# Leading products of a two-layer encoder kernel on x without token factors, splits in landing order, norms written tile by tile

## The chip, the cores and the metric

The kernel runs on one core of a Trainium2 chip. The metric is the device time of one execution in microseconds (us), the median of several. The core has five engines, each with a queue of its own: TensorE (PE; weight loads are shown apart as PEld), VectorE (DVE), ScalarE (ACT), GpSimd (POOL) and SyncE (SP, which here only issues DMAs). SBUF is the on-chip memory, PSUM the accumulators that TensorE writes.

## The reference

Two encoder layers on x, 512 tokens of 1024 channels, in float32. What matters here is the start of each layer:

```
mem_n = rms_norm(mem, mem_norm_g)                      # 256 memory tokens
for l in range(2):
    h = rms_norm(x, g_pre_mix[l])                      # x * rsqrt(mean(x*x) + eps) * g
    proj = h @ w_in[l]                                 # 1024 x 5632
    q_a, k_a, v_a, q_b, k_b, v_b, q_m, gate_pre = split(proj)
    o_a = neighborhood_attention(q_a, k_a, v_a, rpb[l])      # 6 heads
    o_b = dilated_attention(q_b, k_b, v_b)                   # 6 heads
    o_m = memory_attention(q_m, mem_n, w_mem_kv[l])          # 4 heads; kv = mem_n @ w_mem_kv
    merged = sum of three gated branch projections
    x = x + rms_norm(merged @ w_out[l], g_post_mix[l])
    h = rms_norm(x, g_pre_ffn[l])
    u = depthwise_conv(h @ w_up[l]); a, b = split(u)
    x = x + rms_norm((gelu(a) * b) @ w_down[l], g_post_ffn[l])
```

rms_norm is a product of one factor per token (the reciprocal root, "token factor" below), one per channel (g) and x. The token factor can be applied before a product or to its result, since a product with weights mixes channels and not tokens.

## The kernel before, in words

**Layout.** x lies in SBUF transposed, as eight tiles of 128 channels x 512 tokens (`x[k]`), and is worked on in two halves of 256 tokens (`HALVES`). Every product is three matmuls: each operand is split into a high part (fp32r, a ScalarE cast) and the remainder, the low part (a subtraction), and hi·hi, lo·hi and hi·lo are summed in PSUM (`mm3`, all products at L242). In the trace a weight is `wraw` (as loaded, three buffers), `whi` and `wlo` (two buffers each) or, for the leading products, tiles `m`. All operations of ScalarE and VectorE go through one helper and so carry line L114; they are told apart by the names of their tiles. GpSimd's own subtractions are L220, the weight DMAs L225.

**Order of the work.** TensorE's order is fixed by hand: the class `Woven` (L46) chains each matmul behind the one before. Pieces of the kernel are generators ("jobs"), spawned with a delay on a modelled TensorE clock; between products `tick` runs the jobs that are due, `give` and `need` set and await flags, so a job's matmuls fall between the products of the main line. The other engines work off their queues in the order that a scheduler derives; an operation that waits holds up all behind it on its engine.

**The start of layer 0** (L834 to L870). `load_x` (L190) brings half 0 of x in four DMAs, then two weights, then half 1. `first_squares` (L825) has ScalarE square the tiles and VectorE add them; `rstd_job` (L321) turns the sums into token factors: matmuls with `mean` (128x1, into `pt`), a root on ScalarE, a reciprocal on VectorE, and matmuls with `ident` that spread the factors over 128 partitions of a PSUM bank. `pre_norm_job` (L359) then makes eight normed tiles of a half (`normed`, L340: x · g · factor, then the split into `h`) and gives one flag for all eight. `run_group` (L466) multiplies with the six leading weights `FIRST = (0, 3, 6, 1, 4, 7)`, two by two, half 0 and then half 1, into six PSUM banks: mm, mm, s, s, o, pt (288 matmuls of 256 columns).

**Behind it.** `mem_kv` (L444) multiplies the normed memory tokens (`mem_norm_job`, L416, which also needs `mean`, a root and a spread) by four weights, 96 matmuls, with two copies of the results each. Then the loop over `pr`: for pr 0 and 1 the six results of the group are evacuated by `a_q`, `a_k`, `a_v` (L528 to L549: scale and split into `m`, into the padded key tiles `ka`, and into the value tile `sq`), for pr = 2 three more projections (`proj`, L480) are made. `attention_job` (L731) weaves the heads in between. PSUM has three mm banks, two s, two pt and one o.

**The boundary between the layers.** `end_job` (L373) finishes layer 0 half by half: residual adds and square sums per tile, then, after a pause of 9.0, `pre_norm_job` of layer 1. `run_group` of layer 1 waits for the flag of the whole half.

Of the kernel before, what the change touches and what calls it, by code (L numbers as in the profile page):

```python
# [7 lines left out]
F32 = mybir.dt.float32  # L8
# [111 lines left out]
def tile_hybrid_encoder(ctx, tc, xT, memT, memg, vecs, rpb, w_in, w_kv, w_bra, w_brb, w_brm,  # L120
# [18 lines left out]
    def nm(s):  # L139
        uid[0] += 1  # L140
        return f"{s}_{uid[0]}"
# [48 lines left out]
    def load_x(half):  # L190
        for k in range(0, KD, 2):
            nc.sync.dma_start(out=xs[k // 4][:, k % 4:k % 4 + 2, half], in_=xT[:, k:k + 2, half])

    load_x(HALVES[0])
    eps = const.tile([128, 1], F32, name="eps")
    nc.gpsimd.memset(eps, RMS_EPS)
    ACT.activation(smalls(1), eps, AF.Sqrt)
# [21 lines left out]
        last_copy[0] = ACT.copy(hi, src).ins  # L219
        last_lo[eng or V] = (eng or V).tensor_sub(lo, src, f32(hi)).ins  # L220

    def weights(src, K, C, slot=None, eng=None, after=None):

        raw = wp.tile([128, K, C], F32, tag="wraw", name=nm("wraw"))
        nc.sync.dma_start(out=raw, in_=src)  # L225
        if slot is None:
            hi = wp.tile([128, K, C], F32R, tag="whi", name=nm("whi"), bufs=2)
            lo = wp.tile([128, K, C], F32R, tag="wlo", name=nm("wlo"), bufs=2)
            split(raw, hi, lo, eng)
            behind(last_copy[0], after)  # L230
            return [(hi[:, k, :], lo[:, k, :]) for k in range(K)]
        n = 512 // C
        w = []
        for k in range(0, K, n):
            c = min(n, K - k)
            hi, lo = slot(F32R, (128, c, C)), slot(F32R, (128, c, C))
            split(raw[:, k:k + c, :], hi, lo, eng)
            w += [(hi[:, i, :], lo[:, i, :]) for i in range(c)]
        return w
# [105 lines left out]
    def raw_split(l, goff, k, src, hi, lo):  # L345

        g = vec[:, l, goff + k:goff + k + 1]
# [25 lines left out]
    def end_job(l, goff, og, acc, acc2, i, then, lat, more=()):  # L373
        half, box = HALVES[i], []
        yield lat
        yield from rstd_job([acc[:, half]] + list(more), 256, box)
        for k in range(KD):
            V.tensor_mul(og[k][:, half], og[k][:, half], box[0])
            (G if then is None and i and k in TAILG else V).tensor_add(x[k][:, half], x[k][:, half], og[k][:, half])
            if acc2 is not None:  # L380
                sumsq_add(acc2[:, half], x[k][:, half], k == 0, None, G if k in SQG[goff == V_POSTF] else V)
            else:
                nc.sync.dma_start(out=out[:, k, half], in_=x[k][:, half])
        if then is not None:
            yield 9.0
            yield from then(i)

    def factor_end_job(l, goff, og, acc, acc2, i, nxt):

        half, box = HALVES[i], []  # L390
        gnext, h, R = nxt
        yield ready(1.4)
        yield from rstd_job([acc[:, half]], 256, box)
        for k in range(KD):
            V.tensor_mul(og[k][:, half], og[k][:, half], box[0])
            V.tensor_add(x[k][:, half], x[k][:, half], og[k][:, half])
            raw_split(l, gnext, k, x[k][:, half], h[k][0][:, half], h[k][1][:, half])
# [62 lines left out]
    def group_weights(srcs, engs):  # L460
        return [weights(s, KD, 128, big, e) for s, e in zip(srcs, engs)]

    def group_banks():
        return [mmbank(), mmbank(), sbank(), sbank(), obank(128), tbank()]

    def run_group(grp, hs, half, flag, cols=None, side=2):  # L466
        if flag and side == 2:
            wv.need(flag)
        n = len(hs)
        ws, pss = grp  # L470
        for i in range(0, len(ws), side):
            for k in range(n):
                if flag and side > 2:
                    wv.need(f"{flag}.{k}")
                rhs = [t[:, half] for t in hs[k]]
# [356 lines left out]
                V.tensor_add(sqs[k], sqs[k], sqs[k - 2])  # L832
        return sqs[5::2]

    hs = h_tiles()
    wv.spawn(pre_norm_job(0, V_PRE, first_squares(HALVES[0]), hs, 0))
    gw = group_weights([w_in[0, m] for m in FIRST[:2]], (V, G))
    load_x(HALVES[1])
    wv.need(f"h0.{V_PRE}.0")
    with tc.issue_after(last_copy[0]):  # L840
        sqs = first_squares(HALVES[1])
    wv.spawn(pre_norm_job(0, V_PRE, sqs, hs, 1), SD1)
    gw += group_weights([w_in[0, m] for m in FIRST[2:]], (V, G, V, G))
    for t, c in ((mask, c_mask), (tab0, c_tab0), (tab1, c_tab1)):
        nc.sync.dma_start(out=t, in_=c)
    hm = []
    wv.spawn(mem_norm_job(0, hm, big), 6.0)
    km, vm = [], []

    for l in range(depth):  # L850
        pss = group_banks()
        for i in range(2):
            run_group((gw, pss), hs, HALVES[i], f"h{l}.{V_PRE}.{i}")
# [85 lines left out]
        if l == depth - 1:  # L939
            sublayer_end(l, V_POSTF, w_of, fs, 2, None)  # L940
            while wv.jobs:
                wv._step()
        else:
            hm, km, vm = [], [], []
            wv.spawn(mem_norm_job(l + 1, hm, htile))
            box, pre = [], []

            def then(a, i, l=l, box=box):
                if i == 0:
                    box.extend(h_tiles())  # L950
                return pre_norm_job(l + 1, V_PRE, a, box, i)

            gw = []

            def kv_ahead(l=l, pre=pre, gw=gw):
                pre.append(weights(w_kv[l + 1, 0], KD, 128, htile))
                yield KVD
                for i in (1, 2, 3):
                    yield 0.9
                    pre.append(weights(w_kv[l + 1, i], KD, 128, big, G if KVE[i] == 'G' else V))  # L960
                wv.give(f"kv{l + 1}")
                for m in range(NG):
# [9 lines left out]
            wv.need(f"h{l + 1}.{V_PRE}.0")  # L972
            hs = box


# [91 lines left out]
```

## Time and profile before

| | |
|---|---|
| runs | 1562.01, 1562.01 and 1564.1 us, median 1562.01 |
| profiled execution | 1565.1 us, its span 1563.3 us |
| TensorE clock granted | 0.994 of full speed on average |
| TensorE busy | 1524.4 us of the span |
| VectorE, ScalarE, GpSimd busy | 945.2, 735.1, 155.2 us |
| DMA | 144.90 MB, mean 93 GB/s |
| first leading product / last / first pr = 2 projection | 13.66 / 56.49 / 69.59 us |

How to read the views: a line of the timeline gives start, length, engine, line, operation, output<-inputs, shape, and the count of instructions in it; brackets at its end give the idle time of the engine ahead of it and who ended that. A line of the groups gives busy time and the mean length of one instruction in ns. A line of the windows gives the window, its length, then the busy time of PE, PEld, DVE, ACT and POOL with their counts, the granted TensorE clock, the DMA's share and GB/s. Buffer numbers are left out in names.

### The profile page before, as it was taken

What the parts mean: (1) busy time and instruction counts of PE and PEld (TensorE: products, weight loads), DVE (VectorE), ACT (ScalarE), POOL (GpSimd) and SP (SyncE); (2) the same over time, 40 slices, a digit from 0 to 9 for tenths busy, and PEclk for the clock granted to TensorE, in tenths of its full rate; (3) what the DMA queues carried; (4) which work ended last, traced back from release to release, by engine and by line L of the source; (5) the groups of instructions that cost most, each with busy time, mean ns of one, the idle gap of its engine ahead of it and who ended that gap; (6) DMA issues with size and microseconds to landing.
All of it is one profiled execution on the core that took longest, in us unless ns stands there. A gap on an engine that the chain in (4) does not pass through costs nothing.

```text
span 1563.3 us, 20698 instructions
## 1 busy us (share of the span) xinstructions
PE 1524.4 (98%) x7994; PEld 1303.7 (83%) x7994; DVE 945.2 (60%) x1682; ACT 735.1 (47%) x1267; POOL 155.2 (10%) x219
## 2 busy tenths in 40 slices
PE   6999999999999999999989999999999999999997
PEld 6888888888988888788889888888889888888887
DVE  6685566235777777742385856753456877775233
ACT  5564575236544444522344645743364544444231
POOL 4340000210000000100061400001100000000000
PEclk9999999999999999999989999999999999999999
DMA  7222113325113322333331221132250222333331
GB/s 244 88 79 72 61 57 96 93 95 163 54 56 101 100 94 95 104 98 101 115 115 44 80 69 63 56 108 81 95 189 15 81 95 95 94 100 96 98 103 63
DMA packets 46610, 144.90 MB, mean 93 GB/s; under 512 B 5232, under 2 KB 11376, under 8 KB 46512
## 3 DMA queue, kind: packets, MB, share of 16 engines
q1 hardware_dynamic: 44656, 139.61, 28.2%
q10 hardware_dynamic: 1152, 2.10, 0.5%
q0 software_dynamic: 704, 1.88, 0.4%
q8 instruction: 62, 1.02, 0.3%
q14 instruction: 36, 0.29, 0.1%
HBM read 141.47 MB, written 2.10 MB: 92 GB/s over the span
## 4 chain that ended last, share of the span: by engine, by line
PE 54%; DVE 3%; issue 0%; ACT 0%; ACTq 0%; DVEq 0%
PE mm L242 48%; PE s L242 3%; PE o L242 2%; PE pt L242 1%; PE pt L253 1%; DVE y L114 1%; DVE x L114 1%; DVE m L114 0%; DVE acc L114 0%; DVE wlo L114 0%; DVE ka L114 0%; DVE st L114 0%; ACT sq L114 0%; ACT y L114 0%; ACT m L114 0%
## 5 line engine op out<-in xcount | busy, mean ns | idle before, releaser
L242 PE MATMUL mm<-h,whi 128*128 128x512 f32 x2496 | 775.7, 392 | 0.0
L242 PEld LDWEIGHTS mm<-h,whi 128*128 128x128 f32 x2496 | 461.5, 188 | 90.9
L242 PE MATMUL mm<-h,wlo 128*128 128x512 f32 x1248 | 486.4, 390 | 0.0
L114 DVE TENSOR_TENSOR wlo<-wraw,whi 128x1024 fp32r<-128x1024 f32 (+1 forms) x213 | 259.8, 1221 | 293.9 <-ACT whi L114 291.5
L114 ACT CAST whi<-wraw 128x1024 fp32r<-128x1024 f32 (+1 forms) x213 | 221.0, 1039 | 318.5 <-PE mm L242 310.4
L242 PEld LDWEIGHTS mm<-h,wlo 128*128 128x128 f32 x1248 | 234.3, 188 | 49.9
L242 PE MATMUL mm<-m,whi 128*128 128x512 f32 (+1 forms) x800 | 216.3, 358 | 2.7 <-ACT whi L114 1.8
L242 PEld LDWEIGHTS mm<-m,whi 128*128 128x128 f32 x800 | 142.5, 190 | 25.1 <-ACT whi L114 2.2
L242 PE MATMUL mm<-m,wlo 128*128 128x512 f32 (+1 forms) x400 | 142.8, 357 | 1.2 <-DVE wlo L114 1.2
L114 DVE SCALAR_TENSOR_TENSOR y<-y,vec,y 128x511 f32<-128x511 f32 x176 | 130.9, 750 | 3.5 <-ACT y L114 0.9
L114 DVE TENSOR_TENSOR y<-mm,R 128x512 f32<-128x512 f32 x82 | 56.4, 688 | 68.5 <-PE mm L242 68.5
L242 PEld LDWEIGHTS mm<-m,wlo 128*128 128x128 f32 x400 | 75.9, 190 | 12.5 <-DVE wlo L114 1.6
L766 POOL TENSOR_TENSOR m<-m,y 128x512 f32<-128x512 f32 x28 | 36.1, 1288 | 405.7 <-DVE y L114 405.7
L114 ACT ACTIVATE y<-y,vec 128x512 f32<-128x512 f32 x88 | 71.0, 813 | 2.2 <-DVE y L114 1.9
L242 PE MATMUL mm<-m,m 128*128 128x512 f32 x240 | 63.6, 395 | 0.0
L114 ACT ACTIVATE y<-y 128x512 f32<-128x512 f32 x44 | 27.8, 632 | 72.0 <-DVE y L114 71.5
L242 PE MATMUL s<-h,m 128*128 128x256 f32 x384 | 54.7, 290 | 5.4 <-DVE m L114 5.4
L114 ACT ACTIVATE y<-mm,vec 128x512 f32<-128x512 f32 (+1 forms) x91 | 57.4, 631 | 0.1
L242 PE MATMUL mm<-h,m 128*128 128x256 f32 x360 | 54.6, 298 | 2.8 <-DVE h L114 1.8
L114 ACT CAST m<-pt 128x512 fp32r<-128x512 f32 (+1 forms) x72 | 38.2, 539 | 40.4 <-PE pt L253 32.0
L114 DVE TENSOR_TENSOR acc<-acc,sq 128x256 f32<-128x256 f32 (+1 forms) x80 | 40.5, 507 | 26.2 <-ACT sq L114 24.6
L114 DVE TENSOR_TENSOR m<-pt,m 128x512 fp32r<-128x512 f32 (+1 forms) x72 | 45.0, 629 | 18.3 <-ACT m L114 17.4
(143 smaller groups left out, 1762.5 us busy)
## 6 DMA issues: line engine op xcount, KB each, us to landing
wraw<-in_w_in_dram SPq DMA_DIRECT2D x88, 512.0 KB, 3.4
wraw<-in_w_up_dram SPq DMA_DIRECT2D x88, 512.0 KB, 3.3
wraw<-in_w_down_dram SPq DMA_DIRECT2D x32, 512.0 KB, 3.5
wraw<-in_w_out_dram SPq DMA_DIRECT2D x16, 512.0 KB, 4.2
wraw<-in_w_down_dram SPq DMA_DIRECT2D x16, 384.0 KB, 3.1
wraw<-in_w_kv_dram SPq DMA_DIRECT2D x8, 512.0 KB, 4.4
wraw<-in_w_bra_dram SPq DMA_DIRECT2D x16, 192.0 KB, 2.3
x<-in_xT_dram SPq DMA_DIRECT2D x8, 256.0 KB, 6.9
```

The costliest lines, as they stand in the source:

```text
L114: return op(*args, **kw)
L242: wv.pe(nc.tensor.matmul(ps, a, b, start=first, stop=last), cost)
L253: wv.pe(nc.tensor.transpose(ps[:, 128 * i:128 * i + 128], s, ident), 0.11)
L766: (V if br == 2 and m >= 6 else G).tensor_add(acc[m], acc[m], gs)
```

## The change

The change has five parts.

1. **Loads.** The channel factors g of layer 0 come in a small DMA of their own (`g0`, ScalarE's queue). x and the first two weights are loaded in parts: two tiles of x, half of each weight, two tiles of x, the other halves, the last four tiles. The second half of x follows behind the third and fourth weight.
2. **Leading products of half 0 on g · x.** `raw_split` splits x · g without the token factor into `xg`; weights and tiles are split in the order in which they land. The six leading weights are multiplied with `xg` for half 0 and with the normed tiles `h` for half 1. All remainders of the leading weights are VectorE's.
3. **Factors on the outputs.** R is a tile of 128 x 512: 1 for half 1, the token factors for half 0. When the group is done, VectorE multiplies all six results by R (`scaled`) into tiles `y`, and the evacuations read those. The normed tiles of half 0 are still made, later, for all other products. The jobs that make the normed tiles are half 1's at delay 9, half 0's at delay 24.
4. **Memory products later.** In layer 0 `mem_kv` moves behind the pr loop, the memory norm's job starts 10.0 after the group.
5. **Tile by tile.** `pre_norm_job` gives a flag and pauses after each tile, `end_job` likewise, and `run_group` awaits the flag of each tile. At the boundary the next layer's memory norm gets a delay of 20.

```
 def run_group(grp, hs, half, flag, cols=None, side=2):
-        if flag and side == 2:
-            wv.need(flag)
...
-                if flag and side > 2:
+                if flag:
                     wv.need(f"{flag}.{k}")
...
 (pre_norm_job)
-        crit[0] = last_copy[0]
-        yield 1.2
-        wv.give(f"h{l}.{goff}.{i}")
+            crit[0] = last_copy[0]
+            if k == 0:
+                yield 1.2
+            wv.give(f"h{l}.{goff}.{i}.{k}")
+            yield 0.9
...
 (end_job)
+                yield 1.0
...
-            yield 9.0
+            yield 1.0
             yield from then(i)
...
 (start of layer 0)
+    hs, R = h_tiles(), rtile()
+    nc.gpsimd.memset(R[:, HALVES[1]], 1.0)
...
+    for n in range(2):
+        load_x(HALVES[0], (2 * n,))
+        if n == 0:
+            raws = [load_w(w_in[0, m], KD, 128, slice(0, 4)) for m in FIRST[:2]]
+        else:
+            for m, raw in zip(FIRST, raws):
+                load_w(w_in[0, m], KD, 128, slice(4, 8), raw)
+    load_x(HALVES[0], (4, 6))
+    parts = [[], []]
+    for n in range(2):
+        for k in (2 * n, 2 * n + 1):
+            raw_split(g0[:, k:k + 1], x[k][:, HALVES[0]], *xg[k])
+        for part_, raw in zip(parts, raws):
+            hi, lo = big(F32R, (128, 4, 128)), big(F32R, (128, 4, 128))
+            split(raw[:, 4 * n:4 * n + 4, :], hi, lo)
+            part_ += [(hi[:, i, :], lo[:, i, :]) for i in range(4)]
+    for k in range(4, KD):
+        raw_split(g0[:, k:k + 1], x[k][:, HALVES[0]], *xg[k])
+    gw = parts
+    gw += group_weights([w_in[0, m] for m in FIRST[2:4]], (V, V))
     load_x(HALVES[1])
+    wv.spawn(first_norm_job(1, R), 9.0)
+    wv.spawn(first_norm_job(0, R), 24.0)
+    pss = group_banks()
+    run_group((gw, pss[:2]), xg, FULL, None, HALVES[0])
+    gw += group_weights([w_in[0, m] for m in FIRST[4:]], (V, V))
...
+    run_group((gw[2:], pss[2:]), xg, FULL, None, HALVES[0])
+    run_group((gw, pss), hs, HALVES[1], f"h0.{V_PRE}.1")
+    hm, km, vm = [], [], []
+    wv.spawn(mem_norm_job(0, hm, big), 10.0)
...
     for l in range(depth):
+        if l == 0:
+            wv.need(f"h0.{V_PRE}.0.{KD - 1}")
+            pss = [scaled(ps, R) for ps in pss]
...
-        if l == 0:
-            mem_kv(l, hm, km, vm)
...
         for pr in range(3):
             for i, evac in enumerate((a_q, a_k, a_v)):
                 ps = pss[3 * pr + i] if pr < 2 else proj(l, 3 * i + pr, hs, fence if i < 2 else None)
                 evac(ps, qkva, *([f"va{l}.{pr}"] if i == 2 else []))
+        if l == 0:
+            mem_kv(l, hm, km, vm)
...
-            wv.spawn(mem_norm_job(l + 1, hm, htile))
+            wv.spawn(mem_norm_job(l + 1, hm, htile), 20.0)
```

Here `scaled` is `V.tensor_mul(y, ps, R)` on 128 x 512, and `first_norm_job` is squares, `rstd_job`, the copy of half 0's factors into R (ScalarE), then the eight normed tiles with a flag each.

Three places show what this does to the order. The first is VectorE's queue between the last normed tile of the group and the remainders that follow (`y` are the multiplied results, `ka`, `m` and `sq` the evacuated ones, `wlo_719` the remainder of the first pr = 2 weight). After:

```order
L114 TENSOR_TENSOR h_121<-h_98_640,h_120 128x256
L114 TENSOR_TENSOR y_646<-mm_199,R_122 128x512
L114 TENSOR_TENSOR y_648<-s_200,R_122 128x512
L114 TENSOR_TENSOR y_650<-s_201,R_122 128x512
L114 TENSOR_TENSOR y_652<-o_202,R_122 128x512
L114 TENSOR_TENSOR y_654<-pt_203,R_122 128x512
L114 TENSOR_TENSOR m_656<-y_644,m_656 64x512
L114 TENSOR_TENSOR m_657<-y_644,m_657 64x512
L114 SCALAR_TENSOR_TENSOR ka_664<-y_646,ka_662 64x512
L114 SCALAR_TENSOR_TENSOR ka_665<-y_646,ka_663 64x512
L114 COPY sq_682<-y_648 128x8x8 x2
L114 TENSOR_TENSOR m_686<-y_650,m_686 64x512
```

One more `m` and two more `ka` stand behind these, and then `wlo_719`. In before, the same place (`wlo_777` is the remainder of the first memory weight):

```order
L114 COPY sq_872<-s_279 128x8x8 x2
L114 SCALAR_TENSOR_TENSOR ka_884<-o_281,ka_882 64x512
L114 SCALAR_TENSOR_TENSOR ka_885<-o_281,ka_883 64x512
L114 TENSOR_TENSOR wlo_777<-wraw_774,whi_776 128x1024
L114 TENSOR_TENSOR m_724<-mm_698,m_723 64x256 x2
L114 TENSOR_TENSOR wlo_810<-wraw_807,whi_809 128x1024
```

The evacuations read tiles `y` in place of banks, stand in one block behind the six multiplications, and all of them are ahead of the next remainder.

The second place is ScalarE's queue around the root of the memory norm (`st<-pt,eps`). After (`y,st<-y,st` is an exponential of a head, `sq_936` the copy of the pr = 2 value product):

```order
L114 CAST m_870<-pt_865 128x4x64
L114 ACT_TABLE_LOAD
L114 ACTIVATE y_893,st_896<-y_893,st_894 128x256
L114 CAST m_873<-pt_865 128x4x64
L114 ACTIVATE y_893,st_902<-y_893,st_900 128x256
L114 COPY sq_936<-mm_847 128x384
L114 CAST whi_1093<-wraw_1091 128x1024
L114 ACTIVATE y_917,st_920<-y_917,st_918 128x256
L114 ACTIVATE y_917,st_926<-y_917,st_924 128x256
L114 ACT_TABLE_LOAD
L114 ACTIVATE st_943<-pt_940,eps 128x2
```

And before:

```order
L114 ACTIVATE sq_101_407<-m_385 128x256
L114 CAST whi_694<-wraw_692 128x1024
L114 CAST whi_735<-wraw_733 128x1024
L114 ACTIVATE st_545<-pt_542,eps 128x2
L114 ACTIVATE ka_852<-mm_278 64x512
L114 ACTIVATE ka_853<-mm_278 64x512
```

The root stood behind the memory squares and two weight casts; now it stands behind the first exponentials, between two table loads.

The third place is ScalarE's queue ahead of the casts of the third pair of leading weights in after (`y<-x` are squares, `m_254` to `m_268` the casts):

```order
L114 ACTIVATE y_497<-x_85 128x256
L114 ACTIVATE y_498<-x_85 128x256
L114 CAST m_254<-wraw_252 128x512
L114 ACTIVATE y_499<-x_86 128x256
L114 ACTIVATE y_500<-x_86 128x256
L114 CAST m_258<-wraw_252 128x512
L114 ACTIVATE y_501<-x_86 128x256
L114 CAST m_264<-wraw_262 128x512
L114 ACTIVATE y_502<-x_86 128x256
L114 CAST m_268<-wraw_262 128x512
```

In before, casts of the later leading weights stood behind the last squares and around the root of half 1:

```order
L114 ACTIVATE y_219<-x_86 128x256
L114 CAST m_240<-wraw_234 128x512
L114 CAST m_246<-wraw_244 128x512
L114 ACTIVATE st_330<-pt_325,eps 128x2
L114 CAST m_250<-wraw_244 128x512
L114 CAST m_256<-wraw_254 128x512
```

The squares of both halves now stand ahead of and among the third pair's casts.

More of the change, by code (lines that the diff above doesn't have):

```diff
@@ L188, in tile_hybrid_encoder, with load_x @@
     x = [xs[k // 4][:, k % 4, :] for k in range(KD)]
-    def load_x(half):
-        for k in range(0, KD, 2):
+    def load_x(half, ks=range(0, KD, 2)):
+        for k in ks:
             nc.sync.dma_start(out=xs[k // 4][:, k % 4:k % 4 + 2, half], in_=xT[:, k:k + 2, half])
-    load_x(HALVES[0])
+    g0 = const.tile([128, KD], F32, name="g0")
+    nc.scalar.dma_start(out=g0, in_=vecs[:, 0, V_PRE:V_PRE + KD])
     eps = const.tile([128, 1], F32, name="eps")
@@ L220, in split, with load_w, weights @@
         last_lo[eng or V] = (eng or V).tensor_sub(lo, src, f32(hi)).ins
-    def weights(src, K, C, slot=None, eng=None, after=None):
-        raw = wp.tile([128, K, C], F32, tag="wraw", name=nm("wraw"))
-        nc.sync.dma_start(out=raw, in_=src)
+    def load_w(src, K, C, ks=None, raw=None):
+        if raw is None:
+            raw = wp.tile([128, K, C], F32, tag="wraw", name=nm("wraw"))
+        ks = ks or slice(0, K)
+        nc.sync.dma_start(out=raw[:, ks, :], in_=src[:, ks, :])
+        return raw
+    def weights(src, K, C, slot=None, eng=None, after=None, raw=None):
+        if raw is None:
+            raw = load_w(src, K, C)
         if slot is None:
@@ L343, in normed, with raw_split @@
         split(h32, hi, lo, eng)
-    def raw_split(l, goff, k, src, hi, lo):
-        g = vec[:, l, goff + k:goff + k + 1]
+    def raw_split(g, src, hi, lo):
         ACT.activation(hi, src, AF.Copy, scale=g)
@@ L396, in factor_end_job @@
             V.tensor_add(x[k][:, half], x[k][:, half], og[k][:, half])
-            raw_split(l, gnext, k, x[k][:, half], h[k][0][:, half], h[k][1][:, half])
+            raw_split(vec[:, l, gnext + k:gnext + k + 1], x[k][:, half], h[k][0][:, half], h[k][1][:, half])
             if k == 0:
@@ L472, in run_group @@
             for k in range(n):
-                if flag and side > 2:
+                if flag:
                     wv.need(f"{flag}.{k}")
-                rhs = [t[:, half] for t in hs[k]]
+                rhs = [t if half == FULL else t[:, half] for t in hs[k]]
                 for w, ps in zip(ws[i:i + side], pss[i:i + side]):
@@ L833, in first_squares, with first_norm_job @@
         return sqs[5::2]
-    hs = h_tiles()
-    wv.spawn(pre_norm_job(0, V_PRE, first_squares(HALVES[0]), hs, 0))
-    gw = group_weights([w_in[0, m] for m in FIRST[:2]], (V, G))
-    load_x(HALVES[1])
[L839 to L843, printed above, removed]
+    def first_norm_job(i, R):
+        half, box = HALVES[i], []
+        sqs = first_squares(half)
+        yield 2.0
+        yield from rstd_job(sqs, 256, box)
+        if i == 0:
+            ACT.copy(R[:, half], box[0])
+        for k in range(KD):
+            normed(x[k][:, half], g0[:, k:k + 1], box[0], hs[k][0][:, half], hs[k][1][:, half])
+            crit[0] = last_copy[0]
+            if k == 0:
+                yield 1.2
+            wv.give(f"h0.{V_PRE}.{i}.{k}")
+            yield 0.9
@@ new lines, in tile_hybrid_encoder @@
+    hs, R = h_tiles(), rtile()
+    nc.gpsimd.memset(R[:, HALVES[1]], 1.0)
+    xg = [big(F32R, (128, 2, 256)) for _ in range(KD)]
+    xg = [(t[:, 0, :], t[:, 1, :]) for t in xg]
+    gw, raws = [], []
+    hi_lo = [([], []) for _ in range(2)]
+    for n in range(2):
[5 more added lines that the diff above has]
+                load_w(w_in[0, m], KD, 128, slice(4, 8), raw)
@@ L844, in tile_hybrid_encoder @@
+    gw = parts
+    gw += group_weights([w_in[0, m] for m in FIRST[2:4]], (V, V))
+    load_x(HALVES[1])
+    wv.spawn(first_norm_job(1, R), 9.0)
[3 more added lines that the diff above has]
+    gw += group_weights([w_in[0, m] for m in FIRST[4:]], (V, V))
     for t, c in ((mask, c_mask), (tab0, c_tab0), (tab1, c_tab1)):
         nc.sync.dma_start(out=t, in_=c)
-    hm = []
-    wv.spawn(mem_norm_job(0, hm, big), 6.0)
@@ L848, in tile_hybrid_encoder @@
-    km, vm = [], []
+    run_group((gw[2:], pss[2:]), xg, FULL, None, HALVES[0])
+    run_group((gw, pss), hs, HALVES[1], f"h0.{V_PRE}.1")
+    hm, km, vm = [], [], []
+    wv.spawn(mem_norm_job(0, hm, big), 10.0)
     for l in range(depth):
-        pss = group_banks()
-        for i in range(2):
-            run_group((gw, pss), hs, HALVES[i], f"h{l}.{V_PRE}.{i}")
+        if l == 0:
+            wv.need(f"h0.{V_PRE}.0.{KD - 1}")
+            pss = [scaled(ps, R) for ps in pss]
+        else:
+            pss = group_banks()
+            for i in range(2):
+                run_group((gw, pss), hs, HALVES[i], f"h{l}.{V_PRE}.{i}")
@@ L971, in tile_hybrid_encoder @@
             gw += group_weights([w_in[l + 1, m] for m in FIRST[NG:]], [G if e == 'G' else V for e in GEN[NG:]])
-            wv.need(f"h{l + 1}.{V_PRE}.0")
+            wv.need(f"h{l + 1}.{V_PRE}.0.0")
             hs = box
```

## The prediction

> **What bounds the kernel now.** I read the page first: the span, then busy time by engine.
>
> ```profile
> span 1563.3 us, 20698 instructions
> PE 1524.4 (98%) x7994; PEld 1303.7 (83%) x7994; DVE 945.2 (60%) x1682; ACT 735.1 (47%) x1267; POOL 155.2 (10%) x219
> ```
>
> TensorE is busy for all but 38.9 us (1563.3 - 1524.4), and the change neither adds nor removes products. So it can only move those 38.9 us or add to them. The windows, cut at the start, the memory keys and values, the first pr = 2 projections, the attention stretch, and the boundary between the layers, say where they lie (busy time follows each engine's name).
>
> ```profile
> 0.00:56.49 56.49, 43.27 (x320) 42.05 (x321) 39.25 (x82) 29.82 (x71) 24.21 (x52) 1.00 0.58 190
> 56.49:69.59 13.10, 12.18 (x100) 11.83 (x99) 7.17 (x10) 6.38 (x11) 7.34 (x13) 1.00 0.27 91
> 69.59:90.09 20.50, 19.22 (x96) 15.87 (x95) 14.91 (x34) 13.62 (x28) 3.81 (x5) 1.00 0.27 83
> 90.09:650.00 559.91, 557.88 (x2820) 471.38 (x2819) 363.90 (x643) 280.79 (x471) 35.02 (x37) 1.00 0.28 88
> 780.00:820.00 40.00, 33.20 (x250) 32.71 (x249) 34.21 (x75) 19.33 (x48) 26.74 (x48) 0.87 0.37 120
> ```
>
> Idle are 13.2 us of the first 56.5, 0.9 and 1.3 in the next two windows, 6.8 at the boundary, and only 2.0 of the 560 us behind the start. Two consequences: the start and the boundary are what can be won (20 us), and whatever TensorE loses before 90 us can't be taken back in a stretch that idles for 2 us.
>
> TensorE's timeline gives the prices (start, length, count of a group):
>
> ```profile
> 16.08 7.33 PE L242 MATMUL mm<-h,m 128*128 128x256 f32 x41 [1.84 <-DVE h L114]
> 23.50 1.05 PE L242 MATMUL pt<-mean,y 128*128 128x1 f32 x8
> 24.42 0.95 PE L242 MATMUL mm<-h,m 128*128 128x256 f32 x6
> 25.92 0.60 PE L242 MATMUL pt<-ident,st 128*128 128x128 f32 x4
> 26.28 5.28 PE L242 MATMUL s<-h,m 128*128 128x256 f32 x42
> 56.49 0.40 PE L242 MATMUL mm<-m,whi 128*128 128x256 f32 x2
> 812.91 7.13 PE L242 MATMUL s<-h,m 128*128 128x256 f32 x45 [5.37 <-DVE m L114]
> 826.51 5.92 PE L242 MATMUL mm<-h,m 128*128 128x256 f32 x48
> ```
>
> A 256-column product costs 5.92/48 = 0.123 us, and a set of factor matmuls (from 23.50 to 24.42, from 25.92 to 26.28) 1.28 us. The groups run steadily from 16.08 to 56.49. After a 5.4 us wait 45 products took 7.13 us where 5.55 would do: a long wait costs 1.6 us more behind it.
>
> **The start, a gain.** The leading products of half 0 no longer wait for the chain square, mean, root, spread, norm. They need a quarter of x and half of two weights, scaled and split.
>
> ```profile
> GB/s 0 53 353 201 262 354 401 398 345 375 376 360 58 36 273 251 270 304 370 367 104 7 73 371 77 320 182 359 162 126 280 379 353 239 22 0 117 0 15 106
> 3.51 1.42 ACT L114 ACTIVATE y<-x 128x256 f32<-128x256 f32 x4 [1.26 <-DMA x<-in_xT_dram]
> 11.08 1.64 ACT L114 CAST m<-wraw 128x512 fp32r<-128x512 f32 x3
> 20.40 2.56 ACT L114 ACTIVATE y<-x 128x256 f32<-128x256 f32 x8
> 21.25 2.53 DVE L114 TENSOR_TENSOR y<-y,y 128x256 f32<-128x256 f32 x6
> 23.70 0.69 DVE L114 TENSOR_TENSOR m<-wraw,m 128x512 fp32r<-128x512 f32 x1
> wraw<-in_w_in_dram SPq DMA_DIRECT2D x88, 512.0 KB, 3.4
> ```
>
> The first row is what the DMA moved from 0 to 45 us in 40 slices of 1.125 us, the last the page's time from a weight's issue to its landing. x begins to land at 3.5, so I put the first product at 5.5 (before: steady from 16.1). The third weight pair is later: only three raw buffers exist, so the fourth weight is issued behind the second remainder that frees one (about 10.4) and lands 3.4 later, 13.8. Behind it on SP's queue stands x's second half, 1 MB at about 370 GB/s, 2.8 us: 16.6. ScalarE then has the last squares of half 1 (until 17.3) and, mixed with the eight squares of half 0 (0.32 each, 2.56), the four casts of the third pair (0.55 each, 2.2): 22.1. The last remainder (0.69) stands behind two square sums (0.42 each) on VectorE: 23.6. There remain 45 products of half 0 and 144 of half 1 (189 x 0.123 = 23.3) and two factor sets (2.6): group end at 49.5, against 56.49: **-7.0**. Ends: with no such wait 5.5 + 288 x 0.123 + 2.6 = 43.5 (-13.0); with the loads 3 us later 52.5 (-4.0).
>
> Of this, the memory norm's factor set (1.3) and waits of before only change place: they were in the first window, and the 0.9 us idle in the second goes as the memory products move. I set these against each other: 0, within 1.
>
> **S1: the evacuation, uncovered.** In before the memory products (13.1 us) stand behind the group, while VectorE evacuates the six results and makes the next remainder. In after the next PE work behind the group is the pr = 2 projection, and its first remainder stands on VectorE's queue behind all of this: the norm of half 0's eight tiles, six multiplications by R, eight evacuations that now read those products, two copies.
>
> ```profile
> 823.84 1.27 DVE L114 SCALAR_TENSOR_TENSOR h<-x,vec,pt 128x256 f32<-128x256 f32 x3 [1.52 <-PE pt L242]
> 829.17 0.82 DVE L114 TENSOR_TENSOR h<-h,h 128x256 fp32r<-128x256 f32 x2
> L114 DVE TENSOR_TENSOR y<-mm,R 128x512 f32<-128x512 f32 x82 | 56.4, 688 | 68.5 <-PE mm L242 68.5
> 75.44 1.15 DVE L114 TENSOR_TENSOR m<-s,m 64x512 fp32r<-64x512 f32 x2 [0.65 <-ACT m L114]
> L114 DVE COPY sq<-s 128x64 f32<-128x64 f32 x2 | 0.4, 220 | 0.0
> L114 DVE TENSOR_TENSOR wlo<-wraw,whi 128x1024 fp32r<-128x1024 f32 x18 | 22.9, 1276 | 18.3 <-ACT whi L114 18.3
> ```
>
> Norm of eight tiles: 823.84 to 829.99, 6.15 us. Fourteen operations of 0.69, or 0.575 back to back: 8.0 to 9.7. Copies 0.44, remainder 1.28. Together 15.9 to 17.5 from the spread of half 0's factors. That spread is in PE's order 48 products (5.9) ahead of the group's end, and two high-part products (0.5) can go before the remainder is needed: stall 9.5 to 11.1, I take **+10.5**. Only if the factors came much earlier would it vanish.
>
> The norm rows are VectorE's timeline at the second layer's start, undisturbed; the multiplication is the page's group, the copies and remainders those of 40 to 160 us.
>
> The evacuations of before read PSUM and one SBUF tile; now they read two SBUF tiles while GpSimd copies the ka tiles.
>
> ```profile
> 804.30 2.12 DVE L114 TENSOR_TENSOR x<-x,y 128x256 f32<-128x256 f32 x2
> 815.01 0.75 DVE L114 TENSOR_TENSOR x<-x,y 128x256 f32<-128x256 f32 x2
> 803.40 2.74 POOL L220 TENSOR_TENSOR m<-wraw,m 128x512 fp32r<-128x512 f32 x2 [5.44 <-PE s L253]
> 833.62 0.68 DVE L114 SCALAR_TENSOR_TENSOR ka<-mm,ka 64x512 fp32r<-64x512 f32 x1
> 833.32 0.61 POOL L288 CAST ka<-ka 64x512 fp32r<-64x512 f32 x1 [10.27 <-ACT ka L114]
> ```
>
> Two adds with both inputs in SBUF took 2.12 us beside a GpSimd subtraction and 0.75 without; the evacuation from PSUM beside GpSimd's copy kept 0.68. Four copies of 0.61 and one mask subtraction fall into S1; I take **+1.5** (0 to 3). The Trainium skill, "SBUF — State Buffer", § Who interferes with whom, has the rule: a VectorE instruction with two SBUF inputs contends with a GpSimd one that reads SBUF, and the loser blocks for the whole instruction. By that rule the trace agrees (2.12 against 0.75), and S1 would be longer than the evacuation rows of before alone make it.
>
> **S2: the root behind the exponentials.** The memory norm's root comes late. In ScalarE's queue stand ahead of it the evacuations of the projections, four exponentials of head 0, and two table loads. One operand of these, the copy of the pr = 2 value product, can't start before that product ends, and PE has nothing else between its end and the spread of the memory factors.
>
> ```profile
> 81.81 0.37 ACT L114 CAST m<-pt 128x256 fp32r<-128x256 f32 x1 [0.55 <-DVE m L114]
> 82.20 1.28 ACT L114 ACT_TABLE_LOAD   x1
> 83.50 0.51 ACT L114 ACTIVATE y<-y,st 128x256 f32<-128x256 f32 x1
> 83.92 0.19 ACT L114 ACTIVATION_READ_ACCUMULATOR y<-y,st 128x1 f32 x1
> 85.97 1.04 ACT L114 CAST whi<-wraw 128x1024 fp32r<-128x1024 f32 x1
> 91.09 0.48 ACT L114 COPY sq<-mm 128x384 f32<-128x384 f32 x1
> ```
>
> Floor, from that product's end: copy 0.48, weight cast 1.04, two exponentials 1.2, load 1.28, root and reciprocal 0.43: 4.4 us. If ScalarE isn't yet there, it works off five squares, evacuations and casts of the keys, a weight cast, a load and two exponentials besides, by their rows' lengths 12.7 us in all against 6 us of PE work: 6.9. I take **+6.5**: the queue is long, as S1 ends with ScalarE's casts bunched. The load ends at 83.48 and the exponential starts at 83.50. The Trainium skill, "ScalarE: Activation LUTs", § What ACT_TABLE_LOAD costs, speaks against more switches: 1283 ns and about 1380 ns of drain each. By that page S2 would be an estimated 2.8 us longer for its two loads; by the row, which shows the 1.28 alone, it isn't.
>
> **S3: the bank.** Behind the spread PE transposes head 0's values into the PSUM bank that holds the spread memory factors; it comes free with the last of eight normings (823.84 to 829.09 in the like group above, 5.25), less 0.3: **+5.0**, 3.5 to 5.5. In before the memory products themselves stood there, with bank to spare.
>
> **Small.** Waits cool the clock: 1.6 behind S1, 0.4 between, 1.6 behind S3: **+3.6**. One weight remainder **+0.5**. At the boundary, VectorE's work ahead of the last norm is as long as before and starts as before, so the tile flags free nothing: 0.
>
> **Sum.** -7.0 + 10.5 + 1.5 + 6.5 + 5.0 + 3.6 + 0.5 = +20.6. The profiled execution took 1565.1 (span 1563.3), 3.1 above the median of the runs, 1562.01; 1565.1 + 20.6 = 1585.7, and as a median 3.1 lower **1583** (1582.6). A measurement can tell about 0.2%, 3 us.
>
> **The rivals.**
> - *The stalls are given back* (chance 0.10): S1 to S3 lengthen the start, but the attention heads, begun earlier, shorten what follows, and only the gain at the start is left: 1562.0 - 7.0 = 1555. It decides if TensorE waited for the heads' chain for 24 us later; the window from 90 to 650 shows 2.
> - *No change* (0.05): the start runs as fast as products go (-13.0), S1 at its floor (9.5 + 1.6), S2 and S3 hidden by the projections: -1.9, 1560. Against it, nothing stands between the value product and the memory factors.
> - *A faster start only* (0.10): no wait for the third pair, 6.0 less: 1577. For it speaks that DMA could bring all of this in 14 us; against it ScalarE's order.
> - *The boundary is won too* (0.12): normed tiles handed over one by one fill the 6.8 us and spare 1.6 behind: 8.4 less, 1575. For it speaks the 5.37 wait; against it that this wait is for a bank that VectorE frees behind residual adds, not for a tile.
> - *Worse* (0.13): GpSimd blocks VectorE at full price (1.5 more), S1 stands at its upper end (0.6), a further table load falls into S2 (1.3), and the third pair is late (3.0): 6.4 more, 1589. For it speak the adds of 2.12; against it that GpSimd's copies are short.
> - *The forecast* (0.50): 1583.
>
> Range: leaving out the first two and a tail of the worse case leaves 1567 (the won boundary, with the start at its better end) to 1592. Faster by over 0.2%: 0.10; within: 0.05; slower: 0.85.
>
> **What would show it.** In after's timeline: the first product near 5.5, the group's end near 50; then a wait of 10 to 13 us for a wlo, one of 5 to 7 at the memory factors' spread with ScalarE's table load just ahead, one of 5 for a norm at the transposes, and an attention stretch that idles as little as before. The forecast is wrong if the first pr = 2 projection starts within 3 us of the group's end, or if the stretch after 110 us is shorter than before by over 5 us.

## The result, and the profile after

The changed kernel takes 1581.78 us (median of four runs, 1581.4 to 1582.18) against 1562.01 before: a ratio of 1.0109, 95% interval [1.0095, 1.0123]. The forecast was 1583. The profiled execution took 1582.18 us, its span is 1580.4. The two medians alone would give 1.0127 (19.8 us), the two profiled executions 1.0109 (17.1 us). In three later measurements before's median was 1564.63, 1565.87 and 1563.48, which speaks for the smaller figure. All comparisons with after below use 1.0109 and are uncertain by this 0.2% besides their intervals.

Page of after, span and busy time by engine:

```profile
span 1580.4 us, 20704 instructions
PE 1527.9 (97%) x7994; PEld 1306.3 (83%) x7994; DVE 952.5 (60%) x1702; ACT 741.4 (47%) x1278; POOL 147.3 (9%) x214
```

TensorE has the same 7994 instructions and is idle for 52.5 us in place of 38.9. Its busy time is 3.5 us longer too: a product that runs on a cold clock counts as busy for longer (behind the longest wait one took 0.80 us, at 70.18 us the like took 0.39). The windows of after (window, its length, then PE, PEld, DVE, ACT and POOL busy, the granted clock, DMA share, GB/s) say where:

```profile
50.00:70.00 20.00, 7.91 (x23) 5.98 (x24) 14.01 (x18) 6.76 (x11) 12.61 (x15) 0.66 0.21 66
70.00:112.00 42.00, 29.67 (x178) 26.79 (x177) 30.43 (x81) 27.36 (x60) 13.02 (x20) 0.84 0.27 83
112.00:650.00 538.00, 535.89 (x2725) 453.50 (x2725) 344.15 (x605) 268.51 (x451) 30.65 (x32) 1.00 0.28 89
```

From 50 to 112 us TensorE idles for 24.4 us, and the clock averages 0.66 and 0.84, where before's windows there show 1.00. From 112 to 650 it idles 2.1 us, as before: nothing is taken back. TensorE's timeline, the waits in order:

```profile
5.93 1.30 PE L250 MATMUL mm<-m,m 128*128 128x256 f32 x3 [5.93 <-ACT m L114]
8.47 7.99 PE L250 MATMUL mm<-m,m 128*128 128x256 f32 x45 [1.24 <-ACT m L114]
23.78 0.39 PE L250 MATMUL pt<-m,m 128*128 128x256 f32 x1 [0.43 <-DVE m L114]
...
48.58 0.52 PE L250 MATMUL pt<-h,m 128*128 128x256 f32 x3
50.47 0.73 PE L250 MATMUL mm<-h,whi 128*128 128x512 f32 x2 [1.37 <-ACT whi L114]
62.83 0.80 PE L250 MATMUL mm<-h,wlo 128*128 128x512 f32 x1 [11.62 <-DVE wlo L114]
...
91.63 1.22 PE L250 MATMUL pt<-ident,st 128*128 128x128 f32 x4 [6.13 <-DVE st L114]
92.64 1.06 PE L261 MATMUL pt<-ident,y 128*128 128x128 f32 x4
98.27 1.09 PE L261 MATMUL pt<-ident,sq 128*128 128x128 f32 x4 [4.57 <-DVE h L114]
```

The group ends at 49.1 (48.58 + 0.52; before: 56.49). Then come the three waits S1 (11.62, and 1.37 ahead of it), S2 (6.13) and S3 (4.57). What the first is made of stands on VectorE's timeline of after:

```profile
43.79 1.27 DVE L114 SCALAR_TENSOR_TENSOR h<-x,g,pt 128x256 f32<-128x256 f32 x3 [1.92 <-ACT R L114]
...
52.61 0.68 DVE L114 TENSOR_TENSOR y<-pt,R 128x512 f32<-128x512 f32 x1
53.32 1.58 DVE L114 TENSOR_TENSOR m<-y,m 64x512 fp32r<-64x512 f32 x2
54.94 1.70 DVE L114 SCALAR_TENSOR_TENSOR ka<-y,ka 64x512 fp32r<-64x512 f32 x2
56.67 0.59 DVE L114 COPY sq<-y 128x64 f32<-128x64 f32 x2
57.30 2.19 DVE L114 TENSOR_TENSOR m<-y,m 64x512 fp32r<-64x512 f32 x2
59.51 1.71 DVE L114 SCALAR_TENSOR_TENSOR ka<-y,ka 64x512 fp32r<-64x512 f32 x2
61.25 3.07 DVE L114 TENSOR_TENSOR wlo<-wraw,whi 128x1024 fp32r<-128x1024 f32 x2
```

VectorE goes through norm (from 43.79), factors and evacuations without a pause, and only then, at 61.25, begins the remainder that TensorE waits for. And S2 stands on ScalarE's timeline:

```profile
86.57 0.46 ACT L114 COPY sq<-mm 128x384 f32<-128x384 f32 x1
86.92 1.05 ACT L114 CAST whi<-wraw 128x1024 fp32r<-128x1024 f32 x1
...
89.20 0.51 ACT L114 ACTIVATE y<-y,st 128x256 f32<-128x256 f32 x1 [0.72 <-DVE st L114]
89.62 0.19 ACT L114 ACTIVATION_READ_ACCUMULATOR y<-y,st 128x1 f32 x1
89.82 1.28 ACT L114 ACT_TABLE_LOAD   x1
91.11 0.26 ACT L114 ACTIVATE st<-pt,eps 128x2 f32<-128x2 f32 x1
```

TensorE was done with the mean at 85.5; the root runs at 91.11, behind the value copy, a weight cast, the exponentials and the load.

Both kernels share a landmark, the matmuls of `mean` on the residual sums, 56 in seven sets of eight (first and last start behind the durations), before and then after:

```profile
L242 PE MATMUL pt<-mean,acc x56: 165/250/250, 402.5 to 1553.1; 128*128 128x1 f32 x56
```

```profile
L250 PE MATMUL pt<-mean,acc x56: 166/250/250, 424.5 to 1569.4; 128*128 128x1 f32 x56
```

At the first after is 22.0 us late, at the last 16.3: part of what layer 0's start loses is given back behind 402 us, which the forecast had at nothing. The sets between tell where. The second starts at 422.02 and 443.96, the third at 777.56 and 794.28, so some 5.2 us are won between them; only 0.5 is left for the boundary between the layers and what lies behind it. TensorE's waits of after at the boundary (790 to 835 us) are shorter than the 5.4 and 1.4 of before:

```profile
PE mm L250 <- DVE h L114: 3.5, 2, 2.1
PE mm L250 <- ACT h L114: 0.7, 2, 0.4
```

### The profile page after: what moved, and what is told of

Same layout as the page of the kernel before. It is cut to its first block, busy times and chain, and to the rows that moved or that the text cites. A ratio compares the mean times of both kernels' runs of the same rounds, so it can differ in the third digit from the quotient of the medians.

```text
span 1580.4 us, 20704 instructions
## 1 busy us (share of the span) xinstructions
PE 1527.9 (97%) x7994; PEld 1306.3 (83%) x7994; DVE 952.5 (60%) x1702; ACT 741.4 (47%) x1278; POOL 147.3 (9%) x214
## 4 chain that ended last, share of the span: by engine, by line
PE 89%; DVE 4%; ACT 1%; issue 1%; POOL 0%; DMA 0%; ACTq 0%; POOLq 0%; DVEq 0%
PE mm L250 79%; PE s L250 4%; PE o L250 3%; PE pt L261 2%; PE pt L250 1%; DVE m L114 1%; DVE y L114 1%; DVE h L114 1%; DVE ka L114 1%; DVE wlo L114 1%; ACT y L114 0%; DMA m<-in_memT_dram 0%; ACT whi L114 0%; DVE x L114 0%; DVE st L114 0%
## 5 line engine op out<-in xcount | busy, mean ns | idle before, releaser
L250 PE MATMUL mm<-m,m 128*128 128x512 f32 (+1 forms) x288 | 72.9, 389 | 7.2 <-ACT m L114 7.2
L250 PEld LDWEIGHTS mm<-m,m 128*128 128x128 f32 x288 | 52.1, 200 | 16.2 <-ACT m L114 7.5
L114 ACT CAST m<-y 128x512 fp32r<-128x512 f32 (+1 forms) x36 | 22.3, 619 | 72.6 <-DVE y L114 72.5
L114 ACT ACTIVATE y<-y,st 128x256 f32<-128x256 f32 (+1 forms) x80 | 43.7, 547 | 24.9 <-DVE st L114 21.8
```

The lines of the kernel that those rows point to most:

```text
L114: return op(*args, **kw)
L250: wv.pe(nc.tensor.matmul(ps, a, b, start=first, stop=last), cost)
```

## The experiments

Ratios are against the kernel before, measured beside each; 0.1% is 1.6 us. Theory A: the loss is one of order, TensorE's work that covered the evacuation and the root was moved away. Theory B, the rival: the loss is the work that the change adds (multiplications, evacuations from SBUF beside GpSimd, table loads), and would stay in any order.

**Memory norm forward, memory products back ahead of the pr loop** (e1). After, with

```
-    wv.spawn(mem_norm_job(0, hm, big), 10.0)            # behind the group
+    wv.spawn(mem_norm_job(0, hm, big, ktile, 6.0), 0.0) # ahead of half 1's products, raw tiles in ka
...
         fence = crit[0]
+        if l == 0:
+            mem_kv(l, hm, km, vm)                       # and no longer behind the pr loop
```

> The kernel after, with the memory norm brought forward into VectorE's idle stretch before half 0's norm (its raw tiles in ka buffers) and the 96 memory products back between the group and the pr loop. Theory A (order: the loss is the work of TensorE that stood over the evacuation and over the root, and was moved away): the wait of 11.6 us for the first remainder, the 6.1 at the memory factors' spread, the 4.6 at the transposes and some 4.8 of cold clock behind them go, about 2 of small waits stay or come: 1581.8 - 27 = 1555, faster than before by 7. Theory B (work: the loss is what the change adds, multiplications by R, evacuations from SBUF beside GpSimd, table loads): only the waits at the root and the bank go, about 13 with their cold clock: 1569, slower than before.

Measured: 1.0022 [1.0011, 1.0032], so 0.87% less than after. S1, S2 and S3 are gone; the longest wait behind the group is 1.99 us. But it isn't the 0.9955 that 1555 of 1562 us would be: new costs came in at the start. ScalarE's queue shows the memory loads issued while x and the weights were still landing, and the last pair of half 0's x tiles split only when it had landed.

```profile
6.49 0.34 ACTq L430 DMA_DIRECT2D ka<-in_memT_dram  x1
...
13.80 0.91 ACT L114 ACTIVATE m<-x,g 128x256 fp32r<-128x256 f32 x2 [0.80 <-DMA x<-in_xT_dram]
```

In after ScalarE had the high parts of all eight x tiles by 12.3. Besides, the memory squares and two remainders stand among half 1's norms here, and half 0's mean waits 2.6 us for a PSUM bank. The group ends at 59.7, 10.6 later than in after. (Its profiled execution took 1564.33, 4 below its median of 1568.46; what the other executions lost no trace shows.)

**Memory norm forward only** (e2): the same without the second hunk.

> The kernel after, with only the memory norm brought forward; the memory products stay behind the pr loop. Theory A: the waits of 6.1 and 4.6 and the 2.4 of cold clock behind them go, the evacuation stays uncovered (11 to 13 us of wait for the first pr = 2 remainder): 1581.8 - 13 = 1569. Theory B (the extra table loads cost, not the place of the root): two loads of 1.28 less: 1579.

Measured: 1.0083 [1.0070, 1.0097], 0.26% less than after. The waits for the root and the bank are gone, and S1 stands as it was, TensorE's timeline:

```profile
59.98 0.73 PE L250 MATMUL mm<-h,whi 128*128 128x512 f32 x2 [0.25 <-ACT whi L114]
72.32 0.80 PE L250 MATMUL mm<-h,wlo 128*128 128x512 f32 x1 [11.61 <-DVE wlo L114]
```

The time missed the expected 1569 since the early memory norm costs this kernel's start too: its first pr = 2 product starts at 59.98, 9.5 later than in after. Between e1 and e2 only the place of the memory products differs: it is worth 0.61%, 9.5 us, in covering S1.

**Factors multiplied in PSUM** (e3): `V.tensor_mul(ps, ps, R); return ps` in place of the tile y.

> The kernel after, with the six results multiplied by R in their PSUM banks and evacuated from there: as many operations, but no evacuation has two SBUF inputs. Theory A (contention with GpSimd's copies lengthens the block on VectorE by about 2): the wait for the first remainder falls from 11.6 to 9 to 10, 1579.5. Rival (the copies on GpSimd don't matter, the block is only its count of operations): 1581.8, the wait stays 11.6. If writing to PSUM is dearer than writing to SBUF, the wait grows.

Measured: 1.0095 [1.0081, 1.0109], not to be told from after's 1.0109 by time alone. The wait for the first remainder falls from 11.62 to 7.99. The evacuations on VectorE, beside the same GpSimd copies:

```profile
53.56 0.69 DVE L114 TENSOR_TENSOR m<-mm,m 64x512 fp32r<-64x512 f32 x1
54.28 0.68 DVE L114 SCALAR_TENSOR_TENSOR ka<-mm,ka 64x512 fp32r<-64x512 f32 x1
...
58.16 1.21 DVE L114 TENSOR_TENSOR wlo<-wraw,whi 128x1024 fp32r<-128x1024 f32 x1
```

Each takes 0.68 to 0.69; in after two took 1.58 to 2.19. The eight together took 7.2 in after, 5.5 here: 1.7 us for the two SBUF inputs. That agrees with the rule given in the prediction from the Trainium skill's "SBUF — State Buffer", § Who interferes with whom. The other part of the shorter wait is order: here the remainder (58.16) stands ahead of the last two evacuations. Of the 3.6 us, the waits behind took back some (the transposes of the value tile waited 3.2, in after 1.6).

**No factors at all** (e8): `pss = [scaled(ps, R) for ps in pss]` left out, so half 0's token factors are missing from the six results.

> The kernel after without the six multiplications by R, evacuated straight from PSUM (it leaves out the token factors of half 0's leading products). Theory A (VectorE's block behind half 0's norm is what TensorE waits for): the block is shorter by six operations of 0.64 and by 2 of contention: the wait for the first remainder falls from 11.6 to about 6, 1576. Rival (the wait is for something else, the DMA of that weight or ScalarE's cast): it stays near 11.

Measured: 1.0062 [1.0047, 1.0078]. TensorE's timeline:

```profile
52.92 0.79 PE L250 MATMUL mm<-h,wlo 128*128 128x512 f32 x1 [1.24 <-DVE wlo L114]
...
80.56 0.90 PE L261 MATMUL pt<-ident,y 128*128 128x128 f32 x3 [4.90 <-DVE y L114]
```

The wait for the first remainder is 1.24 us; more than expected goes, since without the multiplications most evacuations slip in before half 0's norm. So the wait was for VectorE's block, not for the load or the cast of that weight. But 4.9 of it comes back at head 0's transposes, which now wait for VectorE's softmax.

**Memory loads behind the third pair's casts** (e5): e1 with the four loads issued apart, and half 0's factors where after has them.

```
+    with tc.issue_after(last_copy[0]):
+        mraws = mem_raws(ktile)
+    wv.spawn(mem_norm_job(0, hm, big, mraws, 3.0), 13.0)
```

> As the run with the memory norm forward and the memory products ahead of the pr loop, but the four memory loads are issued behind the casts of the third weight pair, so that they don't take the DMA from x and the weights, and the factors of half 0 come 24 after the start job as in after. In that run the second pair of x tiles was split only at 13.8 us (after: 8.5) and the group ended some 6 us later. Theory A (order) with the loads as the cause of the rest: the group ends near 50 to 52, no wait over 3 us behind it up to 110 us, 1556 to 1559, faster than before by 3 to 6. Theory B (the work added on VectorE keeps the path long whatever the order): waits of together 8 us or more stay between 49 and 110 us, 1562 to 1566.

Measured: 0.9973 [0.9962, 0.9984], 21 us less than after with the same multiplications and evacuations from SBUF. Of the table loads, 31 in before and 33 in after, the two more are gone with the order; at 1.28 us each they are 2.6 of the 21. Theory B falls as the account of the 21 us. One wait over 2 us is left between 45 and 650 us:

```profile
47.24 1.02 PE L250 MATMUL pt<-mean,y 128*128 128x1 f32 x8 [2.55 <-DVE h L114]
```

Half 0's mean waits for the bank of the memory factors. (The group ended at 58.1, not at 50 to 52 as expected: the loads were but a part of what e1 lost at its start, and the memory squares and remainders among half 1's norms are still there. The x tiles that the expectation calls the second pair, split at 13.8 in e1, are the last; the second was split at 9.28 there.)

**Half 0's factors later** (e9): e5 with `wv.spawn(first_norm_job(0, R), 26.0)` in place of 24.0.

> As the run with the memory loads behind the third pair's casts (0.9973 of before), with the job that makes half 0's factors 26 after its spawn in place of 24. There TensorE waited 2.5 us at half 0's mean for the bank of the memory factors and ran cold behind it. If that wait alone is left of the start's loss: it goes, with some 1.5 of cold clock, and nothing comes behind it: 4 us less, 0.9948 of before, at least as fast as before with the boundary edits alone (0.9959). If VectorE's block (norm of half 0, factors, remainders) sets the pace behind the group anyway, it only moves: the wait for the third memory weight's remainder grows by as much: 0.9973.

Measured: 0.9974 [0.9965, 0.9984], no change. The wait of 2.55 is gone and the group ends at 53.9, 4 us earlier than in e5; yet the first pr = 2 product starts at 69.22, only 1.3 earlier than in e5 (70.53; before: 69.59). As the second theory of the expectation had it, the wait moved to the remainder of a memory weight:

```profile
61.91 0.39 PE L250 MATMUL mm<-m,wlo 128*128 128x256 f32 x1 [1.74 <-DVE wlo L114]
```

The windows of e9, and then of before, show VectorE's load there, and a clock of 0.83 behind this wait:

```profile
50.00:60.00 10.00, 10.00 (x85) 9.90 (x83) 9.10 (x22) 6.61 (x15) 1.53 (x3) 1.00 0.01 2
60.00:70.00 10.00, 8.14 (x53) 7.53 (x51) 9.45 (x15) 5.54 (x10) 9.41 (x11) 0.83 0.37 119
70.00:80.00 10.00, 8.79 (x43) 7.14 (x44) 9.18 (x12) 6.41 (x12) 7.83 (x10) 1.00 0.45 139
```

```profile
50.00:60.00 10.00, 10.00 (x86) 10.00 (x85) 5.46 (x13) 3.42 (x8) 3.31 (x5) 1.00 0.01 2
60.00:70.00 10.00, 9.08 (x73) 8.69 (x72) 5.79 (x8) 5.14 (x10) 4.90 (x9) 1.00 0.39 125
70.00:80.00 10.00, 8.72 (x44) 7.05 (x44) 7.24 (x11) 6.49 (x12) 0.00 (x0) 1.00 0.38 122
```

VectorE is busy 27.7 of these 30 us, in before 18.5. Half 0's norm, which in before is done ahead of its products, and the multiplications lie in the stretch that has the remainders and evacuations anyway. That VectorE sets the pace there is read from the windows; no run took work off it there to prove it.

**The boundary.** Three kernels on before's layer 0: only the delay of layer 1's memory norm, `wv.spawn(mem_norm_job(l + 1, hm, htile), 20.0)` (e4); only the tile flags and short pauses of `pre_norm_job`, `end_job` and `run_group` (e6); both (e7, repeated as e10). And after without the delay (e11).

> The kernel before, with only the delay of 20 for layer 1's memory norm. In the profile of before TensorE waits 1.8 + 1.2 us near 663 us for a weight whose cast stands behind the memory squares on ScalarE, and runs cold for about 1.9 behind it; in after both are gone. Theory A (the delay removes it): 3 to 5 us less than before, 1557 to 1559. Rival (the wait belongs to the profiled execution alone, which was 3.1 above the median): 1562, no change.

> The kernel before, with only the tile flags and the shorter pauses at the boundary between the layers (layer 0's start and the memory norm's delay as in before). My forecast said they free nothing: 1562, the 5.4 us wait for the s bank stays. Rival (the boundary is won by the flags): the wait of 5.4 and the 1.4 go, waits of together 4 to 5 for normed tiles take their place and the clock stays warm: 2 to 4 us less, 1558 to 1560.

> The kernel before, with both boundary edits (tile flags, and the delay of 20 for layer 1's memory norm), layer 0 untouched. If the two are independent, their gains add: the delay's 4 us or so and whatever the flags alone give; 1555 to 1558. If the start of layer 0 were the source of the gain that the trace of after shows behind 650 us (6 us), this run would show none of it: 1562.

> The kernel before with both boundary edits, once more, on the same chip as the other two of this group: 0.9959 of before again, and so within 2 us of the run with the factors later if the whole start of after, mended, is worth nothing against the start of before; 2 us or more slower than it if the mended start is worth something.

> The kernel after without the delay of 20 for layer 1's memory norm. If the delay's gain is the same there as in before (5 us), this is that much slower than after: 1.0140 of before, with a wait near 680 us for a weight's cast. If the start's changes had removed that wait on their own: 1.0109 as after.

| | ratio | 95% interval |
|---|---|---|
| before + delay (e4) | 0.9968 | [0.9957, 0.9980] |
| before + flags (e6) | 0.9993 | [0.9983, 1.0002] |
| before + both (e7) | 0.9959 | [0.9946, 0.9971] |
| the same again (e10) | 0.9967 | [0.9954, 0.9980] |
| after (measured apart) | 1.0109 | [1.0095, 1.0123] |
| after without the delay (e11) | 1.0144 | [1.0128, 1.0161] |

The delay is worth 0.32% (5.0 us) in before and 0.35% in after (by the spans of the profiled executions 4.1 and 4.9 us): no dependence on the start shows. What it removes stands in TensorE's timeline of before, and again in that of e11:

```profile
663.26 0.74 PE L242 MATMUL mm<-m,whi 128*128 128x512 f32 x2 [1.81 <-ACT whi L114]
665.20 0.50 PE L242 MATMUL mm<-m,wlo 128*128 128x512 f32 x1 [1.20 <-DVE wlo L114]
```

```profile
685.24 0.73 PE L250 MATMUL mm<-m,whi 128*128 128x512 f32 x2 [1.81 <-ACT whi L114]
687.17 0.79 PE L250 MATMUL mm<-m,wlo 128*128 128x512 f32 x1 [1.20 <-DVE wlo L114]
```

In after, and with the delay in before, neither is there. They stand in the traces of before, e6 and e11 alike, and so are no accident of one execution. The flags alone can't be told from no change. TensorE's waits between 650 and 830 us, of before and of e6, show an exchange at the boundary itself:

```profile
PE s L242 <- DVE m L114: 5.4, 1, 5.4
PE pt L242 <- DVE acc L114: 1.4, 1, 1.4
```

```profile
PE mm L242 <- DVE h L114: 4.0, 2, 2.6
PE mm L242 <- ACT h L114: 0.7, 2, 0.4
```

e10 (0.9967) and e9 (0.9974) ran beside each other: after's whole start, mended, is worth nothing against before's start. The fastest kernel of this study is before with the two boundary edits, 0.3 to 0.4% under before (with the delay alone it can't be told from this), and faster than after by some 1.4 to 1.5% (the two were measured on different occasions, each against before).

## Why the prediction was right, point by point

- **Start, -7.0.** The group ends 7.4 earlier: the size was right, the reason only in part. The wait for the third pair that was to cost 6 cost 0.7 (its last remainder was done at 24.7, forecast 23.6, but TensorE came there no earlier than 22.2). It came late because the first pair was slow: 5.93 to the first product, a wait of 1.24, and 45 products in 7.99 where 5.55 do when warm.
- **S1, +10.5 and +1.5.** From the group's end to 62.83 are 13.7 us, less 0.5 of ready work: 13.2. The contention was 1.7 (e3), as forecast (1.5). Missed was the cast of the weight's high part, which stands behind the last normed tiles on ScalarE: 1.37. e1 against e2, and e8, show that it is the uncovered block.
- **S2, +6.5, and S3, +5.0.** 6.13 and 4.57; both vanish when the norm comes earlier (e2). In the working of S2, 12.7 less 6 is 6.7 and not 6.9; the 6.5 taken is below either. The drain of about 1.4 us with each table load, which the Trainium skill's "ScalarE: Activation LUTs", § What ACT_TABLE_LOAD costs, adds, isn't seen here: the instruction ahead ends at 89.81, the load runs from 89.82 to 91.10, and the root starts at 91.11.
- **Cold clock, +3.6.** Too small. From 62.83 to 68.33 thirteen products took 5.5 us where 3.0 would do (three took 0.70 in before's timeline from 69.59 to 70.29); the spread, the two sets of transposes, the head's scores and the first twelve memory products behind S2 and S3 lost some 3.0: together 5.5.
- **Small terms.** The +0.5 for one more weight remainder shows as no wait of its own in after. A wait of 1.64 at the transposes of the value tile (79.45) was not costed.
- **Nothing taken back.** The rival by which the heads win the time back fell: 2.1 us idle from 112 to 650.
- **The signs.** By its letter one sign of being wrong came true: the first pr = 2 projection starts at 50.47, 1.4 behind the group's end. But the forecast itself let two high-part products go first, and TensorE stops behind them for 11.62, so the sign was ill chosen. The other sign, a stretch after 110 us shorter by over 5, is on the edge: 22.0 late at 402 us, 17.1 at the end of the span.
- **Boundary, 0: the step that failed.** By 402 us the forecast was +20.6 and +22.0 was measured; then after gains 5.7, some 5.2 of it ahead of the boundary itself. The prediction looked at the flags, for which 0 was right (e6), and never costed the delay of 20, although before's trace shows the wait of 1.8 and 1.2 at 663 us that it removes. That is the wait and its cold clock, 5 us in e4. The rival "the boundary is won too" had the right sign for the wrong reason.
- **From profile to median.** The forecast was +20.6 on either. The profiled executions differ by 17.1 (1582.18 - 1565.1), the medians by 19.8: before's profiled execution lies 3.1 above its median, after's 0.4. That 1583 came within 1.2 of 1581.78 is luck: of the missed gain of 5.7, 1.4 was made up by start costs that were too low, 0.8 came in behind the last landmark, and 2.7 lay between profile and median, that is in which four executions of before were measured. The mechanism of the start is what was right; by the profiled executions the sum was 3.5 too high.

## What to carry to other kernels

Work that is moved away from a place covered something there: ask of each moved block which chain on the other engines ran beneath it, and price that chain uncovered, cold clock included; here the order, far more than the added operations, was worth 21 us. An earlier group end is worth only what the engines behind it can follow: in e9 VectorE, 60% busy on average in after, had 2.3 us to spare in 30 at the place that counted. And cost every edit of a diff, the one-number ones too: a single delay, 0.3%, was the only lasting gain in this change.

## What the runs showed of the hardware that was not expected

- At the start the windows of after give a clock of 1.00 from 5 us on, but the pace says otherwise: 45 products from 8.47 on took 7.99 us, and 48 at full pace 5.92. From 9.6 to 13.2 us they started 0.21 us apart, and from 13.6 us on 0.12, in one step. At 100.0 to 101.9 us, where the clock reads 0.50, products of the same width started 0.21 us apart too (nine in 1.92). So the clock column seems to be wrong ahead of its first change; that is inferred from the pace, no run tests it.
- In S1 the clock went to 0.50 about 3.2 us into the wait (0.71 in the slice from 54 to 55 us, the wait began at 51.2) and came back 5.2 us after work resumed (0.96 from 68 to 69 us). Behind the 5.4 us wait of before, at 812.91, it came back after some 3.4 (0.85 from 816 to 817).
